# The state-space output product in three passes, four of its second parts subtracted on GpSimd; four banks for the turned tiles at the begin

## Chip, core and metric

The kernel runs on one core of one Trainium2 chip. The metric is the device time of one execution in microseconds (us). All times of the profile are counted from the start of its span.

## The reference, cut to what matters

Two transformer blocks on 256 tokens of width 1024, all in float32. The part that the change touches is the first block:

```python
h = layer_norm(x, ln_in_g, ln_in_b)
u_glu, z, xbc, dt_raw, gate_a, gate_b = split_in(h @ w_in[l])
y_a = conformer_branch(u_glu, ...)      # a * sigmoid(g), causal conv of 31 taps, layer norm, silu, @ w_conv_out
y_b = ssd_branch(z, xbc, dt_raw, ...)   # state-space scan, gated rms norm, @ w_ssm_out (2048 x 1024)
mix = (sigmoid(gate_a) * y_a + sigmoid(gate_b) * y_b) @ w_o[l]
h = layer_norm(DN_ALPHA * h + mix, ln1_g[l], ln1_b[l])
```

Behind it come a convolutional feed-forward part, and the second block with attention and a mixture of 32 experts, whose weights (192 MB) are all read.

## The kernel before

**Weights and passes.** All dense weights lie in one stream in the order of use, cut into units of 1 MB (128 partitions x 2048 floats). `stream` (L212) loads a unit from the SyncE queue into one of 5 buffers of the pool `ring`. A product in float32 is made in one of two ways. By default (three passes) `passes` (L270) cuts the unit into two halves of 128x1024; for each half `split` (L259) lets ScalarE cast it to the rounded format fp32r (the first part, `wh`) and VectorE subtract this from the float (the second part, `wl`). The activations have such parts too (`x.h`, `x.l`). Then TensorE (PE) makes h x h and l x h for all k of the half, and after these h x l, the only matmuls that need `wl` (`order`, L293). `wh` and `wl` come from the pool `hl`, four buffers of each. Units that stand in `MODES` with 4 (L1523) are not split at all: PE reads the float weights and the float activations, and does four passes by itself.

**Order of the work.** The program is written once, and a planner sets the order of each engine's instructions from it ahead of the run: an engine gets, of what is ready by the planner's reckoning, what stands earliest in the program. At run time each engine's order is fixed, and an instruction waits for its inputs by semaphores. `tc.issue_after(ins)` puts those instructions of the block that run on the engine of `ins` behind `ins`; those on other engines, and loads on the SyncE queue, are not touched.

**Begin (L540 to L583).** Both halves of x are normalized (`norm_rows`, L387), turned by 16 PE transposes (`to_chan`, L353, four for each pair of k, into banks of the pool `sm`, which has two), and evacuated with gain and bias (`affine_split`, L362: k = 0 and 4 by ScalarE, 2 and 6 by VectorE) into `hTf`. Then `hTf` is split into `hT_ah` and `hT_al` (L554). glu0a, the first unit, is in `MODES`, and reads `hTf`; glu0g, the second, is split, and reads `hT_ah` and `hT_al`.

**The stretch around the output product (L789 to L857).** The result of the state-space part, ynT, is split. `ssm_out(0)` (L795) multiplies it by the units ws0 and ws1 (128 columns each, 16 k). After it in the program stand the taps of the convolution (L665 by `tap`, 31 for each of 8 channel tiles; each is one VectorE instruction that reads `vpad` and `cacc`, both in SBUF; many of them run earlier, as filler). Then the layer norm over channels: the pair sums of `cacc` (L810, L812), the product `cs` with a matrix of ones on PE (L820), the centred squares, `cq` (L831), the power on GpSimd that makes the reciprocal deviation (L249), `crr` (L836), the silu on ScalarE and the split into cT (L843). Then `ssm_out(1)` to `ssm_out(3)` with ws2 to ws7, and the product of cT with wc (L853), with w_o (L861), and so on. Of ws0 to ws7 the first four are in `MODES`.

**Later.** From L1047 on `prefetch` (L508) loads the experts' units into buffers of five pools, as these are opened, and later as each pair of experts is done with its own.

Of the kernel before, what the change touches and what calls it, by code (L numbers as in the profile page):

```python
# [11 lines left out]
F32 = mybir.dt.float32  # L12
# [5 lines left out]
ALU = mybir.AluOpType  # L18
# [171 lines left out]
def block_kernel(ctx, tc, I, out, modes):  # L190
    nc = tc.nc
    V, S, G, PE = nc.vector, nc.scalar, nc.gpsimd, nc.tensor
# [5 lines left out]
    sm = ctx.enter_context(tc.tile_pool(name="sm", bufs=2, space=PSUM))  # L198
    ss = ctx.enter_context(tc.tile_pool(name="ss", bufs=2, space=PSUM))
# [8 lines left out]
    def bank(pool, name):  # L208
        return pool.tile([P, 512], F32, tag="b", name=name)
# [22 lines left out]
    def par(name, i=0, n=1):  # L232
        second, o = PPO[name]
        return (pp2 if second else pp)[:, o + i:o + i + n]
# [7 lines left out]
    def rsqrt(out, in_, scale, eps):  # L242

        n = out.free_size()
        first = V.tensor_scalar(out, in_, scale, eps, op0=ALU.mult, op1=ALU.add).ins
        e = neghalf[:, :n]
        if len(out.shape) == 3:
            e = e.rearrange("p (a b) -> p a b", a=out.shape[1])
        G.tensor_tensor(out, out, e, op=ALU.pow)  # L249
        return first  # L250


    def mode_of(name):
        return modes.get(name, 3)
# [1 line left out]
    sg_pool = dense.enter_context(tc.tile_pool(name="sg", bufs=2, reuse_waits="tile"))  # L256
    ada_pool = sg_pool

    def split(h, l, f):  # L259
        a = S.activation(h, f, AF.Copy)  # L260
        return a.ins, V.tensor_tensor(l, f, h.bitcast(F32), op=ALU.subtract).ins  # L261

    def split_act(a, kt, step=4):
        for k in range(0, kt, step):
            s = slice(k, min(kt, k + step))
            split(a.h[:, s], a.l[:, s], a.f[:, s])

    def act(pool, kt, name, tags=("ah", "al"), f=None):

        return Act(f, *(pool.tile([P, kt, T], F32R, tag=t, name=f"{name}_{t}") for t in tags))  # L270

    def passes(w, name):

        if name in ready:
            return ready.pop(name)[1]
        kt, n = w.shape[1], w.shape[2]
        if mode_of(name) == 4:
            return [(range(kt), range(n), [("f", w)])]
        if kt * n <= HALF:
            cuts = [(range(kt), range(n))]  # L280
        elif "_" in name or n == P:
            cuts = [(range(k, k + kt // 2), range(n)) for k in (0, kt // 2)]
        else:
            cuts = [(range(kt), range(c, c + n // 2)) for c in (0, n // 2)]
        got = []
        for i, (ks, cs) in enumerate(cuts):
            h, l = (hl.tile([P, HALF], F32R, tag=t, name=f"{t}_{name}_{i}")[:, :len(ks) * len(cs)]
                    .rearrange("p (k n) -> p k n", k=len(ks)) for t in ("wh", "wl"))
            split(h, l, w[:, ks[0]:ks[-1] + 1, cs[0]:cs[-1] + 1])
            got.append((ks, cs, [("h", h), ("l", h), ("h", l)]))  # L290
        return got

# [13 lines left out]
    def prepare(name):  # L306

        w, _ = stream(name)
        ready[name] = (w, passes(w, name))
# [40 lines left out]
    def units(name, n):  # L350
        return [f"{name}{j}" for j in range(n)]

    def to_chan(src, evac, name, kt=8):  # L353

        for k in range(0, kt, 2):
            b = bank(sm, f"tr_{name}_{k}").rearrange("p (c t) -> p c t", c=2)
            for c in range(2):
                for t in range(2):
                    PE.transpose(b[:, c, t * P:(t + 1) * P], src(t, k + c), ident)
            evac(k, b)  # L360

    def affine_split(a, scale, bias, name):  # L362

        def evac(k, ps_):
            f = a.f[:, k:k + 2] if a.f is not None else sg_pool.tile([P, 2, T], F32, tag="sg", name=f"f_{name}{k}")
            for c in range(2):
                if k % 4:
                    a.last = V.tensor_scalar(f[:, c, :], ps_[:, c, :], scale(k + c), bias(k + c), op0=ALU.mult, op1=ALU.add).ins
                else:
                    a.act = S.activation(f[:, c, :], ps_[:, c, :], AF.Identity, scale=scale(k + c), bias=bias(k + c)).ins  # L370
            if a.f is None:
                a.act, a.last = split(a.h[:, k:k + 2], a.l[:, k:k + 2], f)
        return evac
# [3 lines left out]
    def mean_rstd(x, name, eps=LN_EPS):  # L377
        st = tmp.tile([P, 2, 6], F32, tag="bnst", name=f"st_{name}")
        for h in range(2):
            V.bn_stats(st[:, h, :], x[:, h * 512:(h + 1) * 512])  # L380
        mv = tmp.tile([P, 2], F32, tag="mv", name=f"mv_{name}")
        V.bn_aggr(mv, st)
        r = tmp.tile([P, 1], F32, tag="rst", name=f"rs_{name}", bufs=4)
        rstd.append(rsqrt(r, mv[:, 1:2], 1.0, eps))
        return mv[:, 0:1], r

    def norm_rows(xn, src, t, name, kind, eps=LN_EPS):  # L387

        x = src[:, t, :]
        if kind == "ln":  # L390
            mean, r = mean_rstd(x, f"{name}{t}", eps)
            if t == 0 and name in ("in", "ln1"):
                nm = tmp.tile([P, 1], F32, tag="nm", name=f"nm_{name}{t}")
                V.tensor_scalar(nm, mean, r, -1.0, op0=ALU.mult, op1=ALU.mult)
                return S.activation(xn[:, t, :], x, AF.Identity, scale=r, bias=nm)
            return V.tensor_scalar(xn[:, t, :], x, mean, r, op0=ALU.subtract, op1=ALU.mult)
        r = tmp.tile([P, 1], F32, tag="rst", name=f"rs_{name}{t}", bufs=4)
        s2 = tmp.tile([P, 1], F32, tag="s2", name=f"s2_{name}{t}")
        squared = S.activation(xn[:, t, :], x, AF.Square, accum_out=s2)
        rstd.append(rsqrt(r, s2, 1.0 / D, NORM_EPS))  # L400
        if t == 0 and name == "n1":
            return r, squared, S.activation(xn[:, t, :], x, AF.Identity, scale=r)
        return r, squared, V.tensor_scalar(xn[:, t, :], x, r, None, op0=ALU.mult)
# [124 lines left out]
    with ExitStack() as e1:  # L528
        b1 = e1.enter_context(tc.tile_pool(name="b1", bufs=1, reuse_waits="tile"))
        hT = act(b1, 8, "hT")  # L530
# [9 lines left out]
        with tc.tile_pool(name="pre", bufs=1, reuse_waits="tile") as pre:  # L540
# [6 lines left out]
            hT.f = pre.tile([P, 8, T], F32, name="hTf")  # L547
            for t in range(2):
                norm_rows(xn0, x_sb, t, "in", "ln")
            to_chan(lambda t, k: xn0[:, t, k * P:(k + 1) * P],  # L550
                    affine_split(hT, lambda k: par("ln_in_g", k), lambda k: par("ln_in_b", k), "h"), "h")

            with tc.issue_after(hT.last), tc.issue_after(hT.act):
                for k in range(0, 8, 2):  # L554
# [76 lines left out]
            for i in range(2):  # L631
                q = rs[:, RSO[f"lambda_q{i + 1}_2"]:RSO[f"lambda_q{i + 1}_2"] + 64]
                k = rs[:, RSO[f"lambda_k{i + 1}_2"]:RSO[f"lambda_k{i + 1}_2"] + 64]
# [42 lines left out]
        with tc.tile_pool(name="grp", bufs=1, reuse_waits="tile") as grp:  # L676
# [18 lines left out]
            def ssd_core(g):  # L695
# [68 lines left out]
                def evac(k, ps_):  # L764
                    for i in range(2):
                        S.activation(ynT.f[:, 4 * g + k + i, :], ps_[:, i, :], AF.Copy, scale=par("ssm_norm_w", 4 * g + k + i))
                to_chan(lambda t, k: yg[:, t, k * P:(k + 1) * P], evac, f"yn{g}", kt=4)

            ssd_in(0)
# [48 lines left out]
        b = bank(sm, "cs")  # L818
# [9 lines left out]
        b = bank(sm, "cq")  # L828
# [5 lines left out]
        b = bank(sm, "crr")  # L834
# [11 lines left out]
        for n, i in ((4, "h"), (5, "l")):  # L846
            w = late.tile([P, 2, UNIT], F32, tag=f"ynT_{i}", name=f"w_ada{n}")
# [21 lines left out]
    with ExitStack() as e2:  # L869
# [3 lines left out]
        prepare("up0a0")  # L873
        h1T = act(b2, 8, "h1T")
        to_chan(lambda t, k: xn1[:, t, k * P:(k + 1) * P],
                affine_split(h1T, lambda k: par("ln1_g", k), lambda k: par("ln1_b", k), "h1"), "h1")
        with tc.issue_after(first.ins), tc.issue_after(h1T.last):
# [9 lines left out]
        for j in range(11):  # L887
# [11 lines left out]
            for b, ps_ in enumerate(banks):  # L899
                o = b2.tile([P, 2, T], F32, tag=f"cv{b}", name=f"cv{b}_{j}", bufs=2)  # L900
                for i in range(2):
                    c = 22 * b + 2 * j + i
# [35 lines left out]
    with ExitStack() as e3:  # L938
# [129 lines left out]
        for i in range(4):  # L1068
# [8 lines left out]
            for t in range(2):  # L1077
                for h in (1, 0):
                    c = slice(128 * i + 64 * h, 128 * i + 64 * h + 64)
# [9 lines left out]
        for i in range(4):  # L1089
# [8 lines left out]
            c = slice(128 * i, 128 * i + 128)  # L1098
# [47 lines left out]
        for j, ps_ in enumerate(gemm_chan(units("pd", 2), odT)):  # L1146
# [3 lines left out]
            h, l = (x.parts[j // 2][:, 2 * (j % 2):2 * (j % 2) + 2] for x in (mgT.h, mgT.l))  # L1150
# [52 lines left out]
    for t, h in ((0, 0), (0, 1), (1, 0), (1, 1)):  # L1203
        b = bank((sm, ss)[t], f"tr_x2_{t}{h}")
# [16 lines left out]
    def gather(p, oh, parts):  # L1221

        xb = [bank(ss, f"xg{p}{h}") for h in range(2)]
        m = None
        for h in range(2):
            for i, x in enumerate(parts):
                for t in range(2):
                    for k in range(4):
                        m = PE.matmul(xb[h][:, k * P:(k + 1) * P], x(t, 4 * h + k), oh[:, t].rearrange("p e c -> p (e c)"),  # L1229
                                      start=(i == t == k == 0), stop=(i == len(parts) - 1 and t == 1 and k == 3)).ins  # L1230
        return xb, m
# [49 lines left out]
    xb0, _ = gather(0, oh0, [lambda t, k: res[:, t, k * P:(k + 1) * P]])  # L1281
# [131 lines left out]
    for p in range(NE // 2):  # L1413
        last = p == NE // 2 - 1
        w = [fetched[12 * p + 2 * i:12 * p + 2 * i + 2] for i in range(6)]
# [17 lines left out]
        for j in range(2):  # L1433
            c = slice(j * T, (j + 1) * T)
# [7 lines left out]
        with after(m):  # L1442
            b = bank(ss, f"ht{p}")
# [14 lines left out]
        with after(m):  # L1458

            b = bank(ss, f"cm{p}")  # L1460
# [59 lines left out]


WSJ = 1
MODES = {n: 4 for n in ("ws0", "ws1", "ws2", "ws3", "wo1_1", "dn1_5", "qm_1", "glu0a0")}  # L1523


# [12 lines left out]
```

## Time and profile before

| | |
|---|---|
| three runs, median (lowest to highest) | 1243.82 us (1243.22 to 1249.37) |
| the profiled execution | 1245.51 us, its span 1243.7 us |
| PE busy, share of the span | 1198.8 us, 96% |
| VectorE (DVE) | 776.1 us, 62% |
| ScalarE (ACT) | 495.6 us, 40% |
| GpSimd (POOL) | 26.1 us, 2% |
| granted TensorE clock, mean | 0.996 of full speed |

How to read it: the shares are means over stages with different limits. Rows of a timeline have the start, the duration, the engine, the source line, the operation, and what it writes and reads; in brackets the idle time before it and who ended that. Rows of windows have for each engine the busy time in that stretch with the count of instructions. Instructions of one engine overlap a little at their ends.

### The profile page before, as it was taken

What the parts mean: (1) busy time and instruction counts of PE and PEld (TensorE: products, weight loads), DVE (VectorE), ACT (ScalarE), POOL (GpSimd) and SP (SyncE); (2) the same over time, 40 slices, a digit from 0 to 9 for tenths busy, and PEclk for the clock granted to TensorE, in tenths of its full rate; (3) what the DMA queues carried; (4) which work ended last, traced back from release to release, by engine and by line L of the source; (5) the groups of instructions that cost most, each with busy time, mean ns of one, the idle gap of its engine ahead of it and who ended that gap; (6) DMA issues with size and microseconds to landing.
All of it is one profiled execution on the core that took longest, in us unless ns stands there. A gap on an engine that the chain in (4) does not pass through costs nothing.

```text
span 1243.7 us, 19468 instructions
## 1 busy us (share of the span) xinstructions
PE 1198.8 (96%) x7881; PEld 875.6 (70%) x7881; DVE 776.1 (62%) x1513; ACT 495.6 (40%) x824; POOL 26.1 (2%) x39
## 2 busy tenths in 40 slices
PE   7999999999999999999999999999999999999895
PEld 6988998998969999875888898544444544444341
DVE  6999999999878989568777666532222233222222
ACT  6446778743426666434445544411111111111111
POOL 0000100100000000001000000000000000000000
PEclk9999999999999999999999999999999999999998
DMA  9635343225867656754993259899999999999993
GB/s 355 242 136 203 113 160 136 102 102 203 344 258 278 237 191 224 279 203 185 331 357 133 105 188 359 354 410 418 419 418 421 419 418 419 420 419 418 419 413 141
DMA packets 51916, 353.01 MB, mean 284 GB/s; under 512 B 6000, under 2 KB 6640, under 8 KB 10224
## 3 DMA queue, kind: packets, MB, share of 16 engines
q1 hardware_dynamic: 51824, 351.75, 72.4%
q8 instruction: 62, 1.02, 0.3%
q14 instruction: 30, 0.25, 0.1%
HBM read 350.68 MB, written 1.05 MB: 283 GB/s over the span
## 4 chain that ended last, share of the span: by engine, by line
PE 51%; DMA 19%; DVE 5%; ACT 2%; issue 1%; POOL 0%; ACTq 0%; SPq 0%; DVEq 0%; POOLq 0%
DMA we<-in_experts 19%; PE pd L1480 5%; PE ps_dn L335 5%; PE pg L1427 4%; PE pu L1427 4%; DVE cacc L665 2%; PE ps_ws L324 2%; PE ps_wo L335 2%; PE ps_wc L324 2%; PE ps_wu L335 2%; PE ps_gm L324 1%; PE acc L1405 1%; PE xg L1229 1%; PE ps_qm L335 1%; PE ps_pd L324 1%
## 5 line engine op out<-in xcount | busy, mean ns | idle before, releaser
L1435 DVE TENSOR_TENSOR hid<-hid,pu 128x256 f32<-128x256 f32 x32 | 12.0, 418 | 195.4 <-PE pu L1427 195.4
L1427 PE MATMUL pu<-we,xg 128*64 128x512 f32 x512 | 117.3, 593 | 6.3 <-DMA we<-in_experts 6.3
L1480 PE MATMUL pd<-we,hdT 128*64 128x512 f32 x512 | 115.5, 600 | 3.6 <-issue 2.4
L1427 PE MATMUL pg<-we,xg 128*64 128x512 f32 x512 | 114.4, 593 | 0.2 <-DMA we<-in_experts 0.2
L665 DVE SCALAR_TENSOR_TENSOR cacc<-vpad,pp,cacc 128x256 f32<-128x256 f32 x240 | 101.2, 476 | 0.0
L1427 PEld LDWEIGHTS pu<-we,xg 128*64 128x64 f32 x512 | 37.8, 137 | 82.5 <-issue 68.5
L1427 PEld LDWEIGHTS pg<-we,xg 128*64 128x64 f32 x512 | 38.3, 137 | 73.0 <-issue 69.4
L1480 PEld LDWEIGHTS pd<-we,hdT 128*64 128x64 f32 x512 | 35.6, 137 | 70.8 <-issue 68.0
L260 ACT ACTIVATE osb<-ob 128x512 fp32r<-128x512 f32 x32 | 20.2, 630 | 127.8 <-DVE ob L1483 127.8
L1447 ACT ACTIVATE hdT<-ht 128x512 f32<-128x512 f32 x16 | 9.6, 597 | 148.1 <-PE ht L1446 148.1
L1251 DVE TENSOR_SCALAR xg<-xg,s,mod 128x128 f32<-128x128 f32 x64 | 22.0, 404 | 63.7 <-PE xg L1229 63.7
L1483 DVE SCALAR_TENSOR_TENSOR ob<-pd,wpl,g 128x512 f32<-128x512 f32 x32 | 24.0, 750 | 45.9 <-PE pd L1480 43.3
L1430 ACT ACTIVATE hid<-pg 128x512 f32<-128x512 f32 x16 | 9.6, 597 | 84.1 <-PE pg L1427 84.1
L488 DVE SCALAR_TENSOR_TENSOR sb_ada<-w_ada,silu_c,sb_ada 128x512 f32<-128x512 f32 x49 | 36.6, 747 | 0.6
L261 DVE TENSOR_TENSOR obl<-ob,osb 128x512 fp32r<-128x512 f32 x32 | 22.2, 693 | 22.3 <-ACT osb L260 22.3
L261 DVE TENSOR_TENSOR wl_dn<-w_dn,wh_dn 128x1024 fp32r<-128x1024 f32 x21 | 25.7, 1223 | 16.6 <-ACT wh_dn L260 16.4
L1229 PE MATMUL xg<-oh,res 128*128 128x128 bf16 (+1 forms) x512 | 35.4, 222 | 0.0
L260 ACT ACTIVATE wh_dn<-w_dn 128x1024 fp32r<-128x1024 f32 x21 | 22.3, 1061 | 31.6 <-PE ps_dn L335 24.5
L335 PE MATMUL ps_dn<-wh_dn,guT_gh 128*128 128x512 f32 x84 | 33.7, 402 | 0.0
L335 PE MATMUL ps_dn<-wh_dn,guT_gl 128*128 128x512 f32 x84 | 33.2, 395 | 0.0
L324 PE MATMUL ps_xs<-hT_al,wh_xs 128*128 128x256 f32 x128 | 32.2, 287 | 0.0
L324 PE MATMUL ps_xs<-hT_ah,wh_xs 128*128 128x256 f32 x128 | 31.4, 281 | 0.0
(847 smaller groups left out, 3197.1 us busy)
## 6 DMA issues: line engine op xcount, KB each, us to landing
we<-in_experts SPq DMA_DIRECT2D x189, 1024.0 KB, 19.9
w_ada<-in_stream SPq DMA_DIRECT2D x22, 1024.0 KB, 6.9
w_dn<-in_stream SPq DMA_DIRECT2D x10, 1024.0 KB, 4.8
w_xs<-in_stream SPq DMA_DIRECT2D x8, 1024.0 KB, 4.9
w_z<-in_stream SPq DMA_DIRECT2D x8, 1024.0 KB, 4.7
w_ws<-in_stream SPq DMA_DIRECT2D x8, 1024.0 KB, 4.8
w_bc<-in_stream SPq DMA_DIRECT2D x4, 1024.0 KB, 4.9
w_ga<-in_stream SPq DMA_DIRECT2D x4, 1024.0 KB, 5.1
```

Source lines behind the costliest of these rows:

```text
L260: a = S.activation(h, f, AF.Copy)
L261: return a.ins, V.tensor_tensor(l, f, h.bitcast(F32), op=ALU.subtract).ins
L324: PE.matmul(o, wp, getattr(x, part)[:, k, :], start=(j == 0), stop=(j == len(m) - 1))
L335: PE.matmul(banks[t], getattr(x, p_)[:, u + k, t * P:(t + 1) * P], wp, start=(u == 0 and j == 0), stop=(u + kt == ktot and j == len(m) - 1))
L488: V.scalar_tensor_tensor(a, w[:, q, :], c, a, op0=ALU.mult, op1=ALU.add)
L665: V.scalar_tensor_tensor(o, vpad[:, i, k:k + T], par("conv_dw_w", i * CK + k), o, op0=ALU.mult, op1=ALU.add)
L1229: m = PE.matmul(xb[h][:, k * P:(k + 1) * P], x(t, 4 * h + k), oh[:, t].rearrange("p e c -> p (e c)"), start=(i == t == k == 0), stop=(i == ...
L1251: V.tensor_scalar(xg[:, k, :], src, s2[:, k:k + 1], mod[:, 24 + k:25 + k], op0=ALU.mult, op1=ALU.add)
L1405: m = PE.matmul(acc[t][h], cm[:, t * P:(t + 1) * P], o[:, h, :], start=False, stop=stop and i == 1)
L1427: m = PE.matmul(pgu[i // 2][64 * e:64 * e + 64, :], xg[:, 4 * (i % 2) + k, 64 * e:64 * e + 64], w[i][e][:, k, :], start=(i % 2 == 0 and k ...
L1480: m = PE.matmul(pd[64 * e:64 * e + 64, :], hdT[:, f, 64 * e:64 * e + 64], w[4 + h][e][:, f, :], start=(f == 0), stop=(f == 3))
L1483: V.scalar_tensor_tensor(o, pd, wpl, g2[:, h, :], op0=ALU.mult, op1=ALU.mult)
```

## The change

`split` gets the engine of its subtraction as an argument; for units in `ON_G` (ws0 to ws3) it is GpSimd. These four leave `MODES`, so that they are cast by ScalarE, subtracted by GpSimd and multiplied in three passes. At the begin the transposes of k = 4 and 6 go into banks of the pool `ss` (two more banks), glu0a's load is issued ahead of `to_chan` in the program, and glu0g's casts and subtractions stand behind the last evacuation on ScalarE and on VectorE, ahead of the split of `hTf`.

```diff
-    def split(h, l, f):
+    def split(h, l, f, eng=V):
         a = S.activation(h, f, AF.Copy)
-        return a.ins, V.tensor_tensor(l, f, h.bitcast(F32), op=ALU.subtract).ins
+        return a.ins, eng.tensor_tensor(l, f, h.bitcast(F32), op=ALU.subtract).ins
...
-            split(h, l, w[:, ks[0]:ks[-1] + 1, cs[0]:cs[-1] + 1])
+            split(h, l, w[:, ks[0]:ks[-1] + 1, cs[0]:cs[-1] + 1], G if name in ON_G else V)
...
-    def to_chan(src, evac, name, kt=8):
+    def to_chan(src, evac, name, kt=8, pools=(sm, sm)):
         for k in range(0, kt, 2):
-            b = bank(sm, f"tr_{name}_{k}").rearrange("p (c t) -> p c t", c=2)
+            b = bank(pools[k // 4], f"tr_{name}_{k}").rearrange("p (c t) -> p c t", c=2)
...
+            prepare("glu0a0")
             to_chan(lambda t, k: xn0[:, t, k * P:(k + 1) * P],
-                    affine_split(hT, lambda k: par("ln_in_g", k), lambda k: par("ln_in_b", k), "h"), "h")
+                    affine_split(hT, lambda k: par("ln_in_g", k), lambda k: par("ln_in_b", k), "h"), "h", pools=(sm, ss))
+            with tc.issue_after(hT.last), tc.issue_after(hT.act):
+                prepare("glu0g0")
...
-MODES = {n: 4 for n in ("ws0", "ws1", "ws2", "ws3", "wo1_1", "dn1_5", "qm_1", "glu0a0")}
+ON_G = ("ws0", "ws1", "ws2", "ws3")
+MODES = {n: 4 for n in ("wo1_1", "dn1_5", "qm_1", "glu0a0")}
```

## Rows read from the trace of the kernel before

**Rows 1.** Head of the page.

```profile
span 1243.7 us, 19468 instructions
```

**Rows 2.** Chain of waits in order of time: start, us, what.

```profile
303.62 16.33 PE ps_ws L324 x138
319.95 22.40 PE ps_wc L324 x192
...
959.91 20.07 DMA we<-in_experts
```

**Rows 3.** Windows: stretch, length, busy PE, PEld, DVE, ACT, POOL; clock, DMA share, GB/s.

```profile
258.00:288.00 30.00, 30.00 (x171) 27.34 (x170) 30.00 (x73) 5.57 (x7) 0.00 (x0) 1.00 0.33 110
```

**Rows 4.** Groups of VectorE by line, 255 to 290 us: busy us, mean ns, idle before.

```profile
L665 DVE SCALAR_TENSOR_TENSOR cacc<-vpad,pp,cacc 128x256 f32<-128x256 f32 x70 | 28.0, 477 | 0.0
...
L663 DVE TENSOR_SCALAR cacc<-vpad,pp 128x256 f32<-128x256 f32 x2 | 0.7, 408 | 0.0
...
L798 DVE SCALAR_TENSOR_TENSOR gate_gb<-gate_gb,ps_ws 128x512 f32<-128x512 f32 x1 | 0.7, 679 | 0.0
```

**Rows 5.** Timeline of PE, 240 to 330 us.

```profile
265.62 26.49 PE L324 MATMUL ps_ws<-ynT,w_ws 128*128 128x256 f32 x122
293.46 1.13 PE L820 MATMUL cs<-pair_cs,ones 128*128 128x256 f32 x4 [1.34 <-DVE pair_cs L812]
...
295.53 0.47 PE L324 MATMUL ps_ws<-ynT_h,wh_ws 128*128 128x256 f32 x1
```

**Rows 6.** Timeline of VectorE, 286 to 360 us.

```profile
289.85 1.22 DVE L261 TENSOR_TENSOR wl_ws<-w_ws,wh_ws 128x1024 fp32r<-128x1024 f32 x1
...
312.17 0.68 DVE L261 TENSOR_TENSOR cT_al<-cacc,cT_ah 128x512 fp32r<-128x512 f32 x1
```

**Rows 7.** Timeline of GpSimd, 60 to 260 us.

```profile
126.33 2.05 POOL L708 TENSOR_TENSOR xh<-xh,rs 128x512 f32<-128x512 f32 x2 [106.83 <-ACT xh L704]
...
189.44 0.55 POOL L249 TENSOR_TENSOR gr<-gr,neghalf 128x1 f32<-128x1 f32 x1 [6.37 <-DVE gr L245]
...
225.81 1.05 POOL L708 TENSOR_TENSOR xh<-xh,rs 128x512 f32<-128x512 f32 x1 [4.03 <-ACT xh L704]
227.24 1.06 POOL L708 TENSOR_TENSOR xh<-xh,rs 128x512 f32<-128x512 f32 x1 [0.39 <-ACT xh L704]
...
249.26 0.72 POOL L249 TENSOR_TENSOR gr<-gr,neghalf 128x1 f32<-128x1 f32 x1 [6.79 <-DVE gr L245]
```

**Rows 8.** Timeline of VectorE, 223 to 231 us.

```profile
226.37 1.03 DVE L757 TENSOR_TENSOR yg<-yg,zs 128x512 f32<-128x512 f32 x1
...
227.93 1.46 DVE L261 TENSOR_TENSOR wl_gb<-w_gb,wh_gb 128x1024 fp32r<-128x1024 f32 x1
```

**Rows 9.** Timeline of VectorE, 122 to 132 us.

```profile
125.67 2.42 DVE L672 SCALAR_TENSOR_TENSOR xsT<-ps_xs,pp,xsT 128x255 f32<-128x255 f32 x6
...
128.61 2.42 DVE L672 SCALAR_TENSOR_TENSOR xsT<-ps_xs,pp,xsT 128x255 f32<-128x255 f32 x6
```

**Rows 10.** Timeline of VectorE, 248 to 253 us.

```profile
249.10 2.06 DVE L665 SCALAR_TENSOR_TENSOR cacc<-vpad,pp,cacc 128x256 f32<-128x256 f32 x5
```

**Rows 11.** Windows near the end; columns as in rows 3.

```profile
1221.00:1224.00 3.00, 1.77 (x8) 0.69 (x10) 0.00 (x0) 0.00 (x0) 0.00 (x0) 0.93 0.27 104
1224.00:1227.00 3.00, 2.32 (x5) 0.23 (x1) 0.64 (x1) 0.00 (x0) 0.00 (x0) 0.50 0.01 3
```

**Rows 12.** Timeline of PE, 1180 to 1243 us.

```profile
1222.23 4.09 PE L1480 MATMUL pd<-we,hdT 128*64 128x512 f32 x11 [2.41 <-issue]
```

**Rows 13.** Timeline of PE, 9 to 21.5 us.

```profile
9.14 1.97 PE L359 MATMUL tr_h<-ident,xn 128*128 128x128 f32 x8 [9.14 <-ACT xn L395]
...
11.92 1.91 PE L359 MATMUL tr_h<-ident,xn 128*128 128x128 f32 x8
...
20.73 0.47 PE L324 MATMUL ps_glu0g<-hT_ah,wh_glu0g 128*128 128x256 f32 x1
```

**Rows 14.** Timeline of VectorE, 9 to 21 us.

```profile
16.06 2.49 DVE L261 TENSOR_TENSOR hT_al<-hTf,hT_ah 128x512 fp32r<-128x512 f32 x4
```

## The prediction

> **What bounds the kernel now.** I read the page's head for the span (1243.7 us; the profiled execution took 1245.51 us, so 1.8 us lie around the span) [rows 1], then the chain of waits, then the stretch around the edit by windows, groups and timelines. The chain shows where a gain can get lost: from 960 us on it is made of expert loads [rows 2], so the last quarter is set by the DMA. These loads go into buffers that the dense part and the earlier pairs free; if the dense part ends X later, the loads start X later. I therefore carry a shift at 300 us to the end one for one.
>
> Around the edit two engines are full at once. From 258 to 288 us PE, and VectorE too, are busy 30.0 of 30.0 us, ScalarE 5.6, GpSimd 0 [rows 3]. VectorE spends that time on the taps of the convolution (L665, 70 in this stretch, read from vpad and cacc, both in SBUF) [rows 4]. PE runs the four units ws0 to ws3 in four passes: 122 matmuls in 26.49 us, 0.216 us each; then it waits 1.34 us for the pair sums of the finished taps before the `cs` product [rows 5]. Only after the taps does VectorE make the first second part of ws4, 289.85 to 291.07 us; the conv's result cT is whole at 312.85 us [rows 6]; the product wc that reads it starts at 319.95 us, right behind ws7 [rows 2]. So the conv chain is 7.1 us ahead of PE when wc starts. This margin is what the change spends.
>
> **The output product in three passes.** PE's saving: 128 matmuls at 0.216 us (27.6 us) become 192 at 0.118 us (138 of them took 16.33 us [rows 2]), 22.7 us. That is 4.9 us less; ws3 is through at 265.6 + 22.7 = 288.3 us.
> ScalarE's new casts: eight of about 1.05 us (8.4 us) into a stretch where it was busy 5.6 of 30 us [rows 3]; hidden. The casts and subtractions wait for wh/wl buffers, four of each, which come free every 2.8 us (a half unit is 24 matmuls) and are filled three halves ahead of use, so PE has some 8 us for one cast and one subtraction: no stall in ws0 to ws3. The stream buffers of ws0 to ws3 come free at the subtraction, earlier than at the last matmul now, so SP's loads of ws5 and later get earlier, never later. On GpSimd the eight subtractions end near 281 us; the power for the conv's rstd behind them is needed at about 302 us or later, so nothing queues there.
>
> GpSimd's subtractions are the cost. No row shows this shape. The nearest is L708, two SBUF operands, 128x512, 1.05 us [rows 7]; doubled for 1024 columns that is 2.1 us; if the first 0.15 us don't scale, 1.95 us. I take 2.1 us.
>
> What such an instruction does to VectorE is in the trace. While L708 ran from 225.81 to 226.86 us, a VectorE product of two SBUF tiles that began at 226.37 us took 1.03 us; the same shape, two SBUF inputs, takes 0.68 [rows 6, 8]. It ends 0.68 us after 226.72 us: it stood still until 0.14 us before GpSimd's end. The subtraction of 227.93 us, beside the L708 of 227.24 to 228.30 us, took 1.46 instead of 1.22 us [rows 6 to 8]: again it moved only from 0.13 us before the end. Six conv taps with one input in PSUM took 2.42 us beside L708 at 126.33 us and 2.42 us after it [rows 7, 9]. So what waits is the VectorE instruction with both inputs in SBUF, and that is the tap of L665. The other side waits too: the 1-element power takes 0.55 us alone, and 0.72 us when it begins at 249.26 us in the middle of a tap of 249.10 to 249.58 us, ending 0.40 us behind it [rows 4, 7, 10]. So GpSimd gets in at the first boundary between two taps, and needs the port from 0.15 us after its start.
> The Trainium skill ("SBUF — State Buffer", Who interferes with whom) says the same more strictly: VectorE with two SBUF inputs against GpSimd reading SBUF is an exclusive lock for the whole instruction. By that rule the eight would hold 16.8 us instead of the 14.5 below, and the end would be 2.3 us later.
>
> Price: 2.1 - 0.15 - 0.14 = 1.81 us of VectorE for each subtraction, eight of them 14.5 us. VectorE has no idle time here [rows 3]; only 1.4 us of its work between 255 and 290 us (the two L663 of 0.7 us, one evacuation that reads PSUM) can run beside GpSimd, some 0.4 us of it by chance: 14.1 us net. Bounds: 0 (VectorE never stands still) and 16.8 us (every subtraction blocks in full).
> The skill's "GPSIMD Engine Reference" (3.1 Elementwise) gives 4497 ns for 2048 columns of two-input fp32; halved, an estimate of 2.25 us, above my 2.1. The sum by it would end 1.2 us later.
>
> **Sum for this stretch.** The first second part of ws4 is then done at 291.07 + 14.1 = 305.2 us. PE is through with ws3 at 288.3 us, does the 16 matmuls of ws4 that need no second part by 290.2 us, and stands 15 us. After it: 176 matmuls x 0.118 = 20.8 us, and what else ran on PE between ws4's start and wc's, (319.95 - 295.53) - 192 x 0.118 = 1.7 us, plus 0.93 us for `cs` [rows 2, 5]: 23.4 us. An idle PE also loses its clock: after a wait of 2.41 us near the end the granted clock was 0.93 from 1221 to 1224 us and 0.50 (1.2 GHz) from 1224 to 1227 us [rows 11, 12]: 0.07 x 3 + 0.50 x 3 = 1.7 us of work lost. No row has a wait of 15 us; I take the same 1.7 us behind it. wc starts at 305.2 + 23.4 + 1.7 = 330.3 us, 10.3 us late. The conv chain alone (cT at 312.85 + 14.1 = 327.0 us) would make it 7.0 us late; that is the lower end of this case.
> Whoever sets VectorE's loss at L finds wc at 291.07 + L + 23.4 (+ 1.7 if PE idles long): no gain and no loss at L = 3.8 us with the clock's share, 0.5 us per subtraction.
>
> **The begin.** PE makes 8 transposes, starts on glu0a, makes 8 more from 11.92 us when banks are free, and glu0g starts at 20.73 us [rows 13]. With four banks the 16 can follow each other: 9.14 + 16 x 0.22 + 32 x 0.216 = 19.6 us, at most 1.1 us sooner. The later two evacuations then come sooner, as they wait neither for a bank nor behind glu0g's split; its two casts (1.05 us each) and subtractions go behind them. VectorE's last part of h ended at 18.55 us [rows 14]; with the reordering it stays within half a microsecond of that, and the matmul that needs it comes after 19.6 us. glu0a's load keeps its place on SP ahead of glu0g's, and glu0g's load is not held by the new order, which binds instructions of ScalarE and VectorE alone; POOL has no instruction in it. I take 0.8 us of the 1.1 (bounds 0 and 1.1; if the moved split were late, up to 0.5 us lost), since not every later wait moves along.
>
> Together +10.3 - 0.8 = +9.5 us: 1255.0 us against the profiled 1245.51 us. The median of the three runs, 1243.82 us, is 1.7 us lower, so for the median 1253.3 us.
>
> **Rivals.**
> 1. VectorE hardly loses (L near 0): GpSimd works in the shadow, ws4 waits only for 291.07 us. wc at 291.07 + 23.4 = 314.5 us, 5.5 us sooner, with the begin 6.3: 1237.5 us. For it: nearly all of GpSimd's rows run beside VectorE without harm. Against it: those rows are PSUM readers or powers; the two that met two-SBUF work stretched it. It decides below 0.5 us per subtraction. 0.15.
> 2. Part of the loss is covered: the planner puts second parts of ws4 and ws5 between the taps, or the subtractions fall beside other work, L of 3 to 9 us: 1238 to 1249 us, about 1244. Against it: now these parts wait for the taps although ws4's load is long there. 0.12.
> 3. The other side of the port starves: GpSimd gets through only after the taps, PE stands at ws0's second part. Its first subtraction ends at 289.9 + 2.1 = 292.0 us; then eight units in three passes (45.3 us less the 1.9 us done) and 2.6 us of the rest: wc near 338 us, with the begin 17 us late, 1261 us. Against it: the power that got in after one tap. 0.05.
> 4. The forecast, VectorE blocked by each subtraction: 1250 to 1257 us. 0.68.
>
> **How the numbers follow.** A measurement of this kernel can tell 0.5%, 6.2 us: faster is below 1237.6, slower above 1250.0. Rival 1 lies on the lower bound: 0.10 faster, 0.05 same. Rival 2: 0.10 same, 0.02 slower. Rival 3: slower. The forecast reaches down to 1250: 0.65 slower, 0.03 same. Sum: faster 0.10, same 0.18, slower 0.72. The range 1240 to 1258 us leaves out rivals 1 and 3, 0.20; the forecast's own is 1250 to 1257.
>
> **What would show it.** Right: taps of 0.48 us become some of 2 us beside GpSimd between 258 and 285 us, the last tap ends near 303 us, PE waits some 15 us for ws4's second part, its clock falls to 0.50 there, wc starts near 330 us, and everything behind it keeps its length. The subtractions' own time shows whether 2.1 us was right. Wrong: taps of unchanged length and wc near 314 us (rival 1); second parts of ws4 among the taps (rival 2); a wait inside ws0 (rival 3). The begin is right if glu0g starts between 19.6 and 20.7 us.

## The result, and the profile after

| | before | after |
|---|---|---|
| median (lowest to highest), six runs each | 1244.78 us (1243.10 to 1249.37) | 1260.10 us (1255.45 to 1260.61) |
| the profiled execution, its span | 1245.51 us, 1243.7 us | 1260.61 us, 1258.9 us |
| granted TensorE clock, mean | 0.996 | 0.987 |

After to before: 1.0107 (95% interval 1.0086 to 1.0127). The change makes the kernel slower, as forecast, but by 15 us instead of 9.5: 1260.1 us lies above the range of 1240 to 1258 (one of the six runs, 1255.45 us, lies inside).

The timeline of GpSimd after (start, duration, engine, line, operation, what it writes and reads, count; in brackets the idle time before it) shows the eight subtractions in one piece:

```profile
259.40 20.89 POOL L261 TENSOR_TENSOR wl_ws<-w_ws,wh_ws 128x1024 fp32r<-128x1024 f32 x8 [9.21 <-ACT wh_ws L260]
```

By the view of the tile wl_ws they took 2.60 to 2.90 us each (median 2.61).

The last taps before, and the timeline of VectorE after, which answers to [rows 4, 6]:

```profile
281.32 8.00 DVE L665 SCALAR_TENSOR_TENSOR cacc<-vpad,pp,cacc 128x256 f32<-128x256 f32 x20
```

```profile
259.93 21.04 DVE L668 SCALAR_TENSOR_TENSOR cacc<-vpad,pp,cacc 128x256 f32<-128x256 f32 x9
280.89 0.73 DVE L666 TENSOR_SCALAR cacc<-vpad,pp 128x256 f32<-128x256 f32 x2
281.54 13.15 DVE L668 SCALAR_TENSOR_TENSOR cacc<-vpad,pp,cacc 128x256 f32<-128x256 f32 x33
294.60 0.68 DVE L801 SCALAR_TENSOR_TENSOR gate_gb<-gate_gb,ps_ws 128x512 f32<-128x512 f32 x1
295.20 10.78 DVE L668 SCALAR_TENSOR_TENSOR cacc<-vpad,pp,cacc 128x256 f32<-128x256 f32 x27
...
307.70 1.22 DVE L261 TENSOR_TENSOR wl_ws<-w_ws,wh_ws 128x1024 fp32r<-128x1024 f32 x1
```

Beside the subtractions VectorE got nine taps done in 21.04 us, one for each subtraction and one more; the 33 behind them took 13.15 us, 0.40 us each. The last tap ended at 289.32 us before and at 305.98 us after. The timeline of PE, and the windows, after (they answer to [rows 3, 5, 11]; columns as there):

```profile
308.97 1.44 PE L324 MATMUL ps_ws<-ynT_h,wl_ws 128*128 128x256 f32 x5 [19.31 <-DVE wl_ws L261]
```

```profile
294.00:309.00 15.00, 0.03 (x1) 0.03 (x1) 15.00 (x35) 0.00 (x0) 0.00 (x0) 0.52 0.00 0
309.00:315.10 6.10, 6.10 (x24) 5.74 (x25) 4.60 (x7) 2.89 (x4) 0.00 (x0) 0.50 0.44 172
...
752.00:759.00 7.00, 7.00 (x34) 7.00 (x35) 3.38 (x6) 1.37 (x2) 0.00 (x0) 0.51 0.63 219
```

PE is through with all that it can do of ws4 near 289.7 us, stands 19.31 us for ws4's second part, and goes on at 309 us at half clock for 6.1 us. And there is a second stretch at half clock, from 752 us, that the profile of before does not have.

Where the 15.2 us of the two spans come from, by the first matmul of each product in both traces (after less before): glu0g -0.4; ws0 -0.7; wc +15.9 (319.8 to 335.7 us); pm, at 718 us before, +16.0; behind od's turned tiles, at wu, +19.6; the end +15.2. So 0.7 us are gained ahead of ws0, 16.6 us lost between ws0 and wc, 3.6 us near 752 us, and 4.4 us regained near the end: there before had a wait of 2.41 us inside a product `pd` and half clock behind it [rows 11, 12]. After, that product runs through in one piece (3.0 of the 4.4 us), and the granted clock is 1.00 from 1240 to 1247 us (the other 1.3).

### The profile page after: what moved, and what is told of

Same layout as the page of the kernel before. It is cut to its first block, busy times and chain, and to the rows that moved or that the text cites. A ratio compares the mean times of both kernels' runs of the same rounds, so it can differ in the third digit from the quotient of the medians.

```text
span 1258.9 us, 19630 instructions
## 1 busy us (share of the span) xinstructions
PE 1198.3 (95%) x7945; PEld 880.1 (70%) x7945; DVE 793.4 (63%) x1513; ACT 503.1 (40%) x832; POOL 49.0 (4%) x47
## 5 line engine op out<-in xcount | busy, mean ns | idle before, releaser
L668 DVE SCALAR_TENSOR_TENSOR cacc<-vpad,pp,cacc 128x256 f32<-128x256 f32 x240 | 118.8, 552 | 0.0
L324 PE MATMUL ps_ws<-ynT_h,wl_ws 128*128 128x256 f32 x128 | 19.5, 294 | 19.3 <-DVE wl_ws L261 19.3
L261 DVE TENSOR_TENSOR wl_dn<-w_dn,wh_dn 128x1024 fp32r<-128x1024 f32 x21 | 25.7, 1223 | 16.6 <-ACT wh_dn L260 16.4
L260 ACT ACTIVATE wh_ws<-w_ws 128x1024 fp32r<-128x1024 f32 x16 | 16.9, 1064 | 42.2 <-DVE wl_ws L261 21.0
```

The source lines that it names most:

```text
L261: return a.ins, eng.tensor_tensor(l, f, h.bitcast(F32), op=ALU.subtract).ins
L324: PE.matmul(o, wp, getattr(x, part)[:, k, :], start=(j == 0), stop=(j == len(m) - 1))
L668: V.scalar_tensor_tensor(o, vpad[:, i, k:k + T], par("conv_dw_w", i * CK + k), o, op0=ALU.mult, op1=ALU.add)
```

## The experiments

Twelve kernels. They are compared in two ways: by the whole time against the runs of the kernel before on the same chip (ratio with its 95% interval), and by the stretch from the first matmul of ws0 to the first of wc in the profile, which leaves out the begin and all that the clock does later. sub_alone, which serves for the length of one instruction, is not in the table.

| kernel | ws0 to wc | last tap ends | whole, median | ratio to before |
|---|---|---|---|---|
| before | 54.2 us | 289.32 us | | |
| changed | 70.8 | 305.98 | 1260.10 us | 1.0107 (1.0086 to 1.0127) |
| begin_only | 53.8 | 287.44 | 1244.06 | 0.9993 (0.9977 to 1.0010) |
| gpsimd_writes | 50.6 | 287.60 | 1236.55 | 0.9934 (0.9913 to 0.9955) |
| half_subs | 61.7 | 297.60 | 1247.92 | 1.0017 (0.9997 to 1.0037) |
| one_unit_gpsimd | 59.1 | 292.76 | 1254.37 | 1.0069 (1.0048 to 1.0091) |
| subs_vectore | 68.4 | 292.59 | 1256.70 | 1.0091 (1.0071 to 1.0112) |
| subs_early | 61.4 | 297.34 | 1249.27 | 1.0018 (1.0001 to 1.0035) |
| ws4_early | 69.6 | 309.16 | 1257.64 | 1.0119 (1.0086 to 1.0152) |
| od_kept | 70.5 | 305.11 | 1257.52 | 1.0080 (1.0051 to 1.0109) |
| begin_od | 53.8 | 287.84 | 1246.54 | 1.0000 (0.9985 to 1.0016) |
| taps_act2 | 52.0 | 291.79 | 1245.70 | 0.9985 (0.9964 to 1.0006) |
| taps_act0 | 53.8 | 286.51 | 1245.68 | 0.9995 (0.9978 to 1.0012) |

**begin_only: the begin alone.**

```diff
-ON_G = ("ws0", "ws1", "ws2", "ws3")
-MODES = {n: 4 for n in ("wo1_1", "dn1_5", "qm_1", "glu0a0")}
+ON_G = ()
+MODES = {n: 4 for n in ("ws0", "ws1", "ws2", "ws3", "wo1_1", "dn1_5", "qm_1", "glu0a0")}
```

> Only the begin of the change (four banks, glu0g's split later); the output product as before, four units in four passes. In the profile after the change glu0g starts 0.4 us sooner (20.3 instead of 20.7 us) and the shift is still 0.4 us at 62 us. Theory (the whole loss is in the output product): 0.3 to 0.8 us faster than before, 1244.2 us against 1244.8. Rival (the begin disturbs later stages, and part of the 15 us is its): slower than before by 2 us or more.

1244.06 us, no change that can be measured. Its profile has glu0g at 19.0 us, 1.7 us sooner than before, the changed kernel only 0.4 us; over the twelve profiles with this begin (sub_alone apart) the first matmul of glu0g lies between 19.0 and 20.5 us, 19.7 on the mean (20.7 before). So glu0g starts about a microsecond sooner. In the whole that is not told from zero, and a loss by the begin is at most 0.1% by the interval: it is no part of the 15 us.

**gpsimd_writes: GpSimd only writes.** GpSimd fills the eight second parts with zeros and reads nothing; these second parts are left out.

```diff
-        return a.ins, eng.tensor_tensor(l, f, h.bitcast(F32), op=ALU.subtract).ins
+        return a.ins, (G.memset(l.bitcast(F32), 0.0) if eng is G else eng.tensor_tensor(l, f, h.bitcast(F32), op=ALU.subtract)).ins
```

> The change, but GpSimd writes zeros into the eight second parts instead of subtracting (the second parts of ws0 to ws3 are left out of the product); order of all engines as after the change. Theory (a GpSimd instruction that reads SBUF and a VectorE one with two SBUF inputs exclude each other): no tap is stretched, the last tap ends at 288 to 289 us, wc starts near 315 us, 4 to 5 us before the kernel before, total near 1240 us (3.4 us more if the clock falls at 752 us again). Rival 1 (the loss comes from the order, the buffers or the semaphores of the three passes): it stays, wc near 335 us, total near 1260 us. Rival 2 (any GpSimd access to SBUF blocks): taps stretched by the writes, about 1 us each, wc near 323 us, total 1248 to 1252 us.

GpSimd and VectorE in this kernel (timelines):

```profile
258.54 0.96 POOL L261 MEMSET wl_ws<- 128x1024 f32 x1 [1.84 <-PE ps_gb L324]
```

```profile
258.94 3.65 DVE L668 SCALAR_TENSOR_TENSOR cacc<-vpad,pp,cacc 128x256 f32<-128x256 f32 x9
262.51 0.73 DVE L666 TENSOR_SCALAR cacc<-vpad,pp 128x256 f32<-128x256 f32 x2
```

The same nine taps take 3.65 us instead of 21.04. All orders are those of the changed kernel, PE's work too; so the subtractions, which read SBUF where the zeros do not, cost VectorE 17.4 us, 2.17 us for each subtraction, and the stretch 20.2 us (70.8 less 50.6). The Trainium skill ("SBUF — State Buffer", Who interferes with whom) says that a VectorE instruction with two SBUF inputs contends with a GpSimd instruction that reads SBUF, and not with one that only writes it: the trace agrees, 0.41 us a tap beside the writes.

**half_subs: half the columns.** After the zeros, GpSimd subtracts the first half of each part only.

```diff
+        if eng is G:
+            n = l.shape[1] // 2
+            G.memset(l.bitcast(F32), 0.0)
+            l, f, h = l[:, :n], f[:, :n], h[:, :n]
```

> As the changed kernel, but GpSimd fills each of the eight second parts of ws0 to ws3 with zeros and then subtracts only the first 512 of its 1024 columns (half of these second parts is left out). The order of the other engines is that of the changed kernel. Theory A (the subtraction holds VectorE for its own length, which grows with its columns): a subtraction of some 1.3 to 1.55 us, VectorE loses some 0.9 to 1.15 us for each instead of 2.2, so the last tap ends near 287.6 + 8 = 295 to 297 us (305.98 in the changed kernel, 287.60 with zeros alone), wc starts at 322 to 324 us instead of 335.7, and the whole takes 1245 to 1249 us. Theory B (the price is a fixed one for each hand-over of the memory, whatever the length): last tap at 302 us or later, wc after 330 us, 1255 us or more.

The tile wl_ws in this kernel, GpSimd's subtractions (least / median / most in ns), then two products of VectorE beside them (L670 here, L666 in the changed kernel) and the write of zeros beside the second:

```profile
L265 POOL TENSOR_TENSOR wl_ws<-w_ws,wh_ws x8: 1302/1383/1722, 259.2 to 277.3; 128x512 fp32r<-128x512 f32 x8
```

```profile
266.47 2.48 DVE L670 TENSOR_SCALAR cacc<-vpad,pp 128x256 f32<-128x256 f32 x2
```

```profile
267.70 1.10 POOL L263 MEMSET wl_ws<- 128x1024 f32 x1
```

A subtraction of 512 columns takes 1.30 to 1.72 us (median 1.38), the last tap ends at 297.60 us, 10.0 us behind gpsimd_writes, of which 0.7 us is the later start of ws0: 9.3 us. Not all of it is the subtractions': the first taps of two channel tiles (L670, one input in SBUF) took 2.48 us, the first 1.45 us beside a subtraction, the second 1.12 us beside the write of zeros; in gpsimd_writes, with no GpSimd work beside them, the two take 0.73 us. Without the 0.7 us of that write it is 1.1 us for each subtraction, half of the 2.17 us for half of the columns. So the loss goes with the length of the instruction (theory A); wc at 326.4 us is 2 us later than I expected, the whole as expected.

**sub_alone: GpSimd's instruction by itself.** Six subtractions of the same shape at the very begin.

```diff
+    alone = [hl.tile([P, HALF], F32R, tag=t, name=f"alone_{i}") for i, t in enumerate(("wh", "wh", "wl"))]
+    for a in alone[:2]:
+        G.memset(a.bitcast(F32), 1.0)
+    for _ in range(6):
+        G.tensor_tensor(alone[2], alone[0].bitcast(F32), alone[1].bitcast(F32), op=ALU.subtract)
```

> As the kernel with the edit of the begin alone (ws0 to ws3 in four passes), but six extra GpSimd subtractions of the same shape (128x1024 minus 128x1024, into a split buffer that nobody reads) at the very begin, where VectorE has little or nothing to do. Only their length is of interest. Theory A (2.61 us in the changed kernel is 2.1 us of work, as forecast from the 512-column rows, and 0.5 us of waiting for the tap under way): 2.0 to 2.2 us each while VectorE is idle. Theory B (the instruction itself is longer than the doubled row): 2.4 to 2.6 us each with VectorE idle; then the forecast's size was wrong by itself and the hand-over costs little.

Three of the six on GpSimd's timeline, and what VectorE did beside them:

```profile
8.18 2.34 POOL L235 TENSOR_TENSOR alone<-alone,alone 128x1024 fp32r<-128x1024 f32 x1
...
13.36 2.36 POOL L235 TENSOR_TENSOR alone<-alone,alone 128x1024 fp32r<-128x1024 f32 x1
...
15.80 3.42 POOL L235 TENSOR_TENSOR alone<-alone,alone 128x1024 fp32r<-128x1024 f32 x1
```

```profile
8.11 2.96 DVE L401 TENSOR_SCALAR xn<-x_sb,mv_in,rs_in 128x1024 f32<-128x1024 f32 x1 [0.55 <-POOL rs_in L254]
12.93 0.99 DVE L373 TENSOR_SCALAR hTf<-tr_h,pp 128x256 f32<-128x256 f32 x2 [1.85 <-PE tr_h L364]
14.63 0.99 DVE L373 TENSOR_SCALAR hTf<-tr_h,pp 128x256 f32<-128x256 f32 x2 [0.71 <-PE tr_h L364]
15.78 1.23 DVE L266 TENSOR_TENSOR wl_glu0g<-w_glu0g,wh_glu0g 128x1024 fp32r<-128x1024 f32 x1 [0.15 <-ACT wh_glu0g L265]
```

The one from 13.36 us ran beside VectorE idle or reading PSUM: 2.36 us. That is between my two theories: of the 2.61 us after, 2.36 is the instruction; the other 0.25 I put down to the wait for the tap under way. The one from 15.80 us began 0.02 us behind a VectorE subtraction, waited until that ended at 17.01 us, and needed 2.21 us from there.

**one_unit_gpsimd: two subtractions instead of eight.**

```diff
-ON_G = ("ws0", "ws1", "ws2", "ws3")
-MODES = {n: 4 for n in ("wo1_1", "dn1_5", "qm_1", "glu0a0")}
+ON_G = ("ws0",)
+MODES = {n: 4 for n in ("ws1", "ws2", "ws3", "wo1_1", "dn1_5", "qm_1", "glu0a0")}
```

> Only ws0 in three passes with its two subtractions on GpSimd; ws1 to ws3 in four passes as before. Theory (2.1 us of VectorE per subtraction, price linear): last tap near 293 us, PE done with ws3 near 291.6 us, waits 2 to 4 us for ws4's second part, no fall of the clock, wc near 319 to 320 us: within 1 us of before, 1243.5 to 1245.5 us. Rival (the price is a threshold, paid as soon as GpSimd takes part): 5 us or more slower than before.

The product `cs` on PE:

```profile
296.89 2.07 PE L823 MATMUL cs<-pair_cs,ones 128*128 128x256 f32 x4 [5.48 <-DVE pair_cs L815]
```

Here I was wrong by some 10 us. VectorE's loss is as in the changed kernel: the last tap 5.3 us behind begin_only, 1.0 us of it a later start, so 2.2 us for each subtraction. But PE's order has `cs` ahead of ws4's second parts, so it waited 5.48 us (1.34 us before [rows 5]), lost its clock in that wait (0.50 from 295 to 300 us), and the stretch is 59.1 us. So it is no threshold of GpSimd: at `cs` the taps had no margin at all, PE waited for their sums before too. The other half of the excess came later: 36.0 us from pm's first matmul to wu's instead of 32.8, and the end.

**subs_vectore and subs_early: VectorE makes its second parts itself.** First only the engine, then with ws2 and ws3 ahead of the taps in the program.

```diff
-ON_G = ("ws0", "ws1", "ws2", "ws3")
+ON_G = ()
...
-WSJ = 1
+WSJ = 2
```

(subs_vectore has the first of the two edits, subs_early both. `WSJ` is the number of pairs of units whose products stand ahead of the taps in the program.)

> The change with the eight subtractions on VectorE instead of GpSimd (8 x 1.13 = 9.0 us more in its queue). Theory: VectorE loses 9.0 us instead of 17.0; last tap near 298 us, second part of ws4 near 300 us, PE waits about 10 us and its clock falls, wc near 326 us, total 1251 to 1253 us: GpSimd costs 8 us more than doing the work on VectorE itself. Rival (what costs is three passes with their second parts at all, wherever they are made): same as after the change, 1260 us.

1256.70 us, between the two expectations. PE waits 16.61 us inside ws2, until 294.39 us: the taps stand ahead of ws2 in the program, so the planner put the last four subtractions behind all of them. The run says nothing on who should subtract; subs_early does:

> All eight subtractions on VectorE, and the products of ws2 and ws3 moved ahead of the taps in the program (two double units instead of one), so that all eight subtractions stand between taps when TensorE needs them; with VectorE's subtractions before, four of them stood behind the last tap and TensorE stopped inside ws2. Theory A (a subtraction costs VectorE its own 1.14 us if VectorE makes it, and 2.2 us if GpSimd does; the place did the rest): the last tap ends at 287.6 + 9.1 = 296.7 us (305.98 with GpSimd), TensorE does not wait before it is through with ws3, wc starts at 321 to 325 us (335.7), the whole takes 1247 to 1251 us. Theory B (the three passes cost the margin of the taps whoever subtracts): wc at 331 us or later, 1256 us or more.

```profile
299.14 2.08 PE L324 MATMUL ps_ws<-ynT_h,wl_ws 128*128 128x256 f32 x8 [10.39 <-DVE wl_ws L261]
```

```profile
288.56 8.78 DVE L668 SCALAR_TENSOR_TENSOR cacc<-vpad,pp,cacc 128x256 f32<-128x256 f32 x22
```

These are PE's wait and VectorE's last taps. PE's wait is at ws4 now and 10.39 us, the last tap ends at 297.34 us, 9.7 us behind gpsimd_writes for eight subtractions: 1.2 us each. So a subtraction costs VectorE 1.2 us if it makes it and 2.17 us if GpSimd does. The whole is 11 us shorter than the changed kernel, with the other order in it too (GpSimd's subtractions with `WSJ` at 2 are in ws4_early: 1.0119). It still does not beat before.

**ws4_early: ws4's second parts between the last taps.**

```diff
-WSJ = 1
+WSJ = 2
...
+        prepare("ws4")
         for j in range(0, 8, 2):
             for k in range(CK):
```

> The changed kernel with ws4 loaded and split ahead of the taps in the program (and ws2 and ws3 with it), so that VectorE makes the two second parts of ws4 between the last taps instead of behind them; GpSimd's eight subtractions as in the changed kernel. Theory A (their place behind the last tap, 307.70 to 308.92 us, is a part of the excess): TensorE does 32 more products of ws4 (3.8 us) within its wait, the pair sums come 2.3 us later, and from the first product of ws0 to the first of wc it takes 68 to 69.5 us instead of 70.8; 1257 to 1259.5 us. Theory B (the wait is for the taps alone, and the place is worth nothing): 70.5 us or more, 1259.5 to 1261 us.

The median is in A's range, the stretch (69.6 us) just outside. But by pm the profile is 16.7 us late, more than the changed kernel: PE starts wc 1.0 us sooner (334.7 us) and starts its last matmul of it 0.7 us later (358.7 for 358.0), since the taps end later and the convolution's result with them. And its stretch from pm to wu is 33.1 us instead of 36.4, which the edit has nothing to do with. Not shown, then, that the place is worth anything to the whole.

**od_kept and begin_od: nine idle matmuls in PE's wait for od's turned tiles**, in the changed kernel and in begin_only.

```diff
-        to_chan(lambda t, k: od[:, t, k, :], evac3, "od", kt=4)
...
+        pm = gemm_chan(units("pm", 2), omT)
+        with tc.issue_after(mlast[0]):
+            keep_warm(9, ss, "od")
+        with tc.issue_after(mlast[0]):
+            to_chan(lambda t, k: od[:, t, k, :], evac3, "od", kt=4)
```

(`mlast[0]` is the last matmul of a product, or of `keep_warm`, which multiplies `ident` by `ident`.)

> The changed kernel with nine idle matmuls (identity by identity, 128 columns, 0.216 us each) behind the last matmul of pm, in the 2 us in which TensorE waits for the turned tiles of od; nothing else in its order changes but the two shw products, which come behind the turning. Theory A (the clock's fall to half from 752 to 759 us comes from this wait and costs 3.6 us): the granted clock stays at 1.00 between 745 and 765 us, everything behind od is 3 to 4 us sooner, and the whole takes 1256 to 1257.5 us. Theory B (the fall has another cause, or comes all the same a little later): 1259 to 1261 us with 3 to 7 us at half clock near there.

The window of od_kept that answers to the last one of after:

```profile
752.00:759.00 7.00, 7.00 (x62) 7.00 (x62) 2.19 (x6) 2.65 (x5) 0.00 (x0) 1.00 0.71 261
```

No fall: from pm's first matmul to wu's 33.6 us instead of 36.4, 0.8 us more than the 32.8 of before; that much is spent on the idle matmuls. The median, 1257.52 us, is at the edge of theory A's range. That the idle matmuls kept the clock is likely, but not shown: six of the twelve profiles without them have no fall at this wait either, and the interval (1.0051 to 1.0109) overlaps the changed kernel's.

> The edit of the begin alone (ws0 to ws3 in four passes) with the same nine idle matmuls ahead of od's turning. If the fall of the clock at od costs the kernel before something in a part of its executions, as it did for 3.41 us in the profile of the begin alone: 1241 to 1243 us, 0.1 to 0.3% below the kernel before, and fewer executions above 1246. If not: 1243.5 to 1245 us as the begin alone.

A miss: 1246.54 us, above both expectations. Its od is free of a fall, but this profile has one behind other, short waits (0.68, 0.56 and 0.22 us) that the edit does not touch (a window of begin_od):

```profile
574.00:578.00 4.00, 4.00 (x11) 2.72 (x11) 4.00 (x10) 2.82 (x4) 0.00 (x0) 0.72 0.98 397
```

In begin_only, which has the same three waits, it is at 1.00. Filling one wait gained nothing here that can be measured.

**taps_act2 and taps_act0: a version that might beat both.** The first tap of each channel tile on ScalarE; taps_act2 has ws0 and ws1 in three passes with VectorE's subtractions, taps_act0 none.

```diff
-                V.tensor_scalar(o, vpad[:, i, 0:T], par("conv_dw_w", i * CK), par("conv_dw_b", i), op0=ALU.mult, op1=ALU.add)
+                S.activation(o, vpad[:, i, 0:T], AF.Identity, scale=par("conv_dw_w", i * CK), bias=par("conv_dw_b", i))
...
+ON_G = ()
+MODES = {n: 4 for n in ("ws2", "ws3", "wo1_1", "dn1_5", "qm_1", "glu0a0")}
```

> A version that may beat both: the edit of the begin; the first tap of each channel tile (a product with gain and bias, one input) on ScalarE instead of VectorE; only ws0 and ws1 in three passes, their four subtractions on VectorE, ws2 and ws3 in four passes. VectorE gets 4 x 1.14 = 4.6 us more and some five taps less between 259 us and the last tap (2.4 us): last tap near 289.7 us; TensorE is through with the first half of ws4 near 291 us, so neither waits long. wc at 315 to 316.5 us (317.5 with the begin alone, 319.8 before), the whole 1241 to 1243 us. Rival (the later waits and the clock take it back, or ScalarE's taps hold up others): 1244 to 1248 us.

> The edit of the begin and the first taps on ScalarE alone, ws0 to ws3 in four passes as before. TensorE sets this stretch (it reaches cs 2.4 us after the taps could), so VectorE's gain is worth nothing: 1243 to 1245 us, as the begin alone (1244.06). Rival (VectorE's time sets it here already): 1241 to 1242.5 us.

taps_act2 shortens the stretch by 1.8 us against begin_only (52.0 for 53.8), but ws0 starts 2.4 us later in its profile, wc at 318.1 us, and the whole, 1245.70 us, is in the rival's range and 0.9985 of before, not told from 1. taps_act0 is no change against before, as expected: its taps end 0.9 us sooner than in begin_only though ws0 starts 1.7 us later, and the stretch is as long. No version that keeps all second parts beats the kernel before by more than the measurement can tell.

## Why the prediction was right in direction and too small

- **The mechanism** held: the forecast's case, the taps blocked one subtraction long each, the chain ws4's second part to PE, the wait, the half clock, wc late. Shown by gpsimd_writes: without GpSimd's reads 20.2 us of the stretch go. PE's saving is there too: with zeros the stretch is 3.6 us shorter than before (54.2 to 50.6), where the forecast saw 4.9 in the matmuls alone.
- **The step that failed first** is the price, "2.1 - 0.15 - 0.14 = 1.81 us of VectorE for each subtraction, eight of them 14.5 us". Measured 2.17 us, 17.4 us in all: +2.9 us. 2.1 was a 512-column row of another operation doubled [rows 7]; the instruction takes 2.36 us undisturbed (sub_alone) and 2.61 between taps. The two sentences on the Trainium skill, 2.25 us by "GPSIMD Engine Reference" (3.1 Elementwise) and the lock by "SBUF — State Buffer" (Who interferes with whom), give together an estimate of 8 x 2.25 = 18.0 us: nearer to the 17.4 than my rows were. That the lock is for the whole instruction, the page says in its words on VectorE's two-port modes.
- **The cover**, "some 0.4 us of it by chance", was nothing. Each of the eight subtractions ran beside a tap; the two L666 came behind GpSimd's end (280.89 for 280.29 us), the evacuation at 294.60 us. Nor can the L663 of before run beside GpSimd, as I took it: half_subs has them at 2.48 us instead of 0.73. By luck this cost nothing: one tap less stood in the stretch (71 for 72). So the last tap is some 17 us later (305.98 less 289.32, and the begin's 0.4), where I had 14.1 us.
- **Behind the last tap** I let ws4's second part follow as before, 0.53 us behind it. The planner put it 1.72 us behind (307.70 less 305.98), after two pair sums and an evacuation: +1.2 us on PE's wait (what moving it is worth to the whole stayed open, ws4_early).
- **The clock's share** was 1.7 us; 6.1 us of work at 0.50 cost 3.1 us: +1.4. The begin gave 0.4 us in this profile instead of 0.8: +0.4. Another 0.3 us between PE's restart and wc is not placed. Together 6.2 us: wc at 335.7 us, forecast 329.5.
- **"Everything behind it keeps its length"** held from wc to pm to 0.1 us (398.6 and 398.7 us) and not after: +3.6 us near 752 us, of which 0.4 us is a longer wait for od's turned tiles (1.86 us for 1.49) and the rest the half clock behind it; -4.4 us near the end, 3.0 of it a wait that is gone and 1.3 the clock. That these two nearly cancel is luck; the sum had neither.
- **The rivals**: GpSimd starved (1261 us) came out nearest to the measured time and is wrong in its cause: GpSimd was through at 280.29 us, taking turns with the taps. VectorE unharmed and partial cover are excluded by the nine taps in 21.04 us.

Open: why the same wait of 1.5 us at od costs the clock in some profiles and not in others (below), and so a few microseconds of any single comparison; and what ended the wait near the end of before, for which the profile shows no releaser [rows 12].

## What to carry to other kernels

Handing a two-input subtraction in SBUF to an idle GpSimd is no help to a VectorE that is full with two-input work in SBUF: it cost VectorE 2.17 us there and 1.2 us at home. Take the price from an instruction of the same shape and count the whole of it against the other engine. And when a change shortens the engine that is not last, ask first what margin the last one has: here PE already waited 1.34 us for the taps' sums [rows 5].

## What the runs showed of the hardware that was not expected

- GpSimd and VectorE, both with work queued, took turns strictly: eight subtractions, one tap between each, 2.6 us for a pair. Neither starved.
- A VectorE product with one SBUF input met GpSimd too: `xn` (128x1024) took 2.96 us beside the subtraction of 8.18 us, and 0.81 us before. The products of `hTf`, which read PSUM, kept their 0.99 us. The products L670 of half_subs, again with one SBUF input, stood beside a mere write of zeros too. The page "SBUF — State Buffer" of the Trainium skill (Who interferes with whom) has this for VectorE's two-port modes; the traces show the standing still (2.96 for 0.81 us, 1.12 for 0.41), not the mode.
- The wait of PE ahead of od's transposes was 1.5 us in before and in nine of the experiments, 1.86 us in the changed kernel and in ws4_early. From pm's first matmul to wu's it took 32.8 us in before, half_subs, sub_alone, taps_act0 and taps_act2, and 33.1 in ws4_early; 34.4 in begin_only and gpsimd_writes; 36.0 in one_unit_gpsimd, subs_vectore and subs_early, 36.4 in the changed kernel. So behind the same wait the clock stayed at 1.00, or fell to 0.50 for a shorter or a longer time.
